# A two-layer trunk of sparse attention, retention and gated ConvFFN on one core: retention's loads a head ahead, the last FFN by the first one's code, and signs on ScalarE in the top-k

## The chip, the cores and the metric

One Trainium2 chip, one of its cores. TensorE (PE) multiplies, VectorE (DVE), ScalarE (ACT) and GpSimd (POOL) work on tiles of 128 partitions, SyncE (SP) issues the DMAs in order. The metric is device time in microseconds (us) from the first to the last instruction of one execution, as the median of several runs. Every product is made of float32 operands split into a high and a low fp32r part (three matmuls: high by high, high by low, low by high).

## The reference

```
for i in range(2):                                    # x: (1, 1024 tokens, 1024)
    h = rms_norm(x, norm_mix_g[i])
    x = x + (dsa_mixer(h) if i == 0 else retention_mixer(h))
    x = x + conv_ffn(rms_norm(x, norm_ffn_g[i]))

dsa_mixer:  proj = h @ w_in -> q (8 heads of 128), c (latent), qi, ki (8 index heads of 64), wi
    score = sum_h wi_h * relu(qi_h . ki), keys of later 64-chunks masked
    idx = top_k(score, 256);  k_sel, v_sel = gathered rms_norm(c), c
    o = softmax(q . k_sel) @ v_sel;   return o @ w_out
retention_mixer:  q, k = rotary(...) (4 heads of 256), v (4 of 512), g
    s = (q . k) * decay within chunks of 64; the state carries k^T v from chunk to chunk
    y = rms_norm(intra + cross) * silu(g);   return y @ w_out
conv_ffn:  u = causal 3-tap conv(h @ w_up) + bias -> a, b (2816 each);  return (silu(a) * b) @ w_down
```

## The kernel before, in words

Tokens are worked in two halves of 512, and activations lie with features on partitions. The large products over all tokens (FFN up, retention's q, k, g and values) are done by a Strassen-like scheme of seven products with operands B (first half) and T1 to T4, B22 (made of both halves by `second_inputs`). The first two products per chunk (`first_products`) need only the first half and can be made early; their results go out to DRAM (`pd`, `rp`) and come back in `second_products`.

Order of the stages: in_proj of half 0 and half 1, attention of query blocks 0 to 3, out_proj, part of the first FFN's first products, attention of blocks 4 to 7, out_proj, the first FFN, retention's inputs (`ret_inputs`: q, k, g by first and second products, then the values), retention half 0 and half 1, the second FFN (`ffn_whole`).

The top-k (L392) finds for each query the 256th largest score. It settles the 31 bits of a threshold from the top: one round counts per block, on DVE, the scores at or above the threshold (L407), then two small instructions set the bit (L417, L418). Top-k "a" is for blocks 2 and 3 (rows of 384 and 512 scores) and runs beside in_proj of half 1; top-k "b" is for blocks 4 to 7 (640, 768, 896, 1024) and runs beside the attention of blocks 0 to 3. Both are generators: other code draws a count or two at each of its own steps (`steps`, L1342, L1352), which sets where the counts stand in DVE's order.

The values (L605 and after, `run`): for each of two pairs of heads five products, each by two halves; a half's weight is summed on DVE, split on ACT and DVE, and multiplied. The loop asks for a weight where it is used.

Retention (L671) is called per half and loops over four heads: q·k (L730), the split of its masked result to sTh and sTl, in half 1 the state's load and split (L745), the output before the norm (rt), in half 0 the new state (L780 to L794), the next head's q and k (`qk`, L796: load through the raw buffers, rotary on DVE, split), transposes (L804) and the swish gate to y (L806), the next head's v (L809), then the head's part of the output product (L817) with weights by `weight()` (L97), which loads two ahead. There are two raw buffers (L84, L680), and q, k, v and weights all take them in turn.

`ffn_whole` makes the first products of four chunks in advance, the rest chunk by chunk. `down` takes its groups and tile places per layer from DOWN; in the first FFN the second half's convolution is done late, by `gate` (L1140).

Of the kernel before, what the change touches and what calls it, by code (L numbers as in the profile page):

```python
# [8 lines left out]
I32 = mybir.dt.int32  # L9
AF = mybir.ActivationFunctionType  # L10
# [5 lines left out]
T = 1024  # L16
# [3 lines left out]
DOWN = (([(0, 4), (4, 6), (10, 6), (16, 6)], (14,)), ([(0, 6), (6, 6), (12, 6), (18, 4)], (0, 12)))  # L20

PRE = (5, 4)
# [3 lines left out]
MASKED = -1.0e30  # L26

# [24 lines left out]
class Prog:  # L52
# [4 lines left out]
    def plan_weights(self, phases):  # L57
        i = self.ins
        seq = []
        for ph, a in phases:  # L60
# [5 lines left out]
            elif ph == "up":  # L66
                seq += [(i["wf_up"][0, c], 1024, True) for c in range(*a)]
            elif ph == "ret":
# [301 lines left out]
    def indexer(self, b, qs, t0, masks):  # L370
# [4 lines left out]
        for h in range(8):  # L375
            for (o, n) in self.segs(L):
# [6 lines left out]
                if h == 0:  # L383
                    nc.vector.tensor_scalar(sc[:, o:o + n], rl[:, :n], w, None, op0=ALU.mult)
# [7 lines left out]
    def topk(self, tag, scs, junk, eqs):  # L392

        nc = self.nc
# [6 lines left out]
        t = thr.bitcast(F32)  # L403

        def count(of, op):
            for b in range(B):
                V.tensor_scalar(junk[:, :Ls[b]], scs[b], of(b), None, op0=op, op1=ALU.add, accum_out=cnt[:, b:b + 1])  # L407
                yield
# [151 lines left out]
    def ret_inputs(self, x, tt, s3, B):  # L560
# [5 lines left out]
        def steps():  # L566
            yield
            yield
            self.mean_square(1)
            yield  # L570
            yield
            chunk = self.normaliser(x[1], C_GMIX + 8, 1)
            yield from self.second_inputs(x[0], x[1], tt, chunk, hold)

        rest = steps()
# [24 lines left out]

        nxt = self.prep_b(self.ret_src(0)[1], self.raw_of(self.ret_src(0)[0]), s3)
        self.second_products(16, self.ret_src, ops, nxt, s3, self.rp, done)

        for vp in range(2):
            vs = [self.hp.tile([128, 2, 2048], F32, tag="h", name="va") for _ in range(2)]  # L605
            (a21, a22), (a11, a12) = [(v[:, 0], v[:, 1]) for v in vs]
            for q in range(2):
                for t, hd, kh in ((a21, 1, 0), (a22, 1, 1), (a11, 0, 0), (a12, 0, 1)):
# [7 lines left out]
            def run(ps, of, tok, first, last, out):  # L616
# [3 lines left out]
                for j in range(4):  # L620
                    out(j, ps[j])
# [847 lines left out]
```

## Time and profile before

| | |
|---|---|
| median of 3 runs | 2869.95 us (2869.47 to 2870.96) |
| the profiled execution | 2871.95 us, span 2870.2 us |
| mean granted TensorE clock | 0.952 of full speed |
| PE busy | 2631.9 us (92%) |
| DVE busy | 2011.2 us (70%) |
| ACT busy | 1134.0 us (40%) |

Windows give the busy time of each engine in a stretch of the span, then PEclk, the granted clock as a share of full speed, and the share of DMA. Waits say which operation an engine stood before, and which engine's result it waited for last. Groups by shape read: line, engine, operation, out<-in, shapes, count | busy us, mean ns of one | idle before, by releaser. Stages by time: in_proj of half 1 from about 97, attention of blocks 0 to 3 from about 242, the first FFN's second part from 680, values 1600 to 1737, retention 1737 to 2194.3, the inputs of the second FFN 2194 to 2260.

### The profile page before, as it was taken

To read this page: it belongs to the slowest core of one execution; us is meant where nothing else is said; L and a number is where in the kernel's file an instruction comes from. 1 tells how busy PE (TensorE), PEld (TensorE's weight loads), DVE (VectorE), ACT (ScalarE), POOL (GpSimd) and SP (SyncE) were. 2 spreads that over 40 slices of the span, in tenths; PEclk is the share of its full clock that TensorE was granted. 3 is DMA by queue.
4 is the path that set the end of the run, shared out by engine and by line. 5 is a ranking of instruction groups with operands and counts; after the bars stand their busy time and mean duration, and the time that the engine had idled before them with its cause. 6 is when DMAs were issued, how large, how long until landed. Compare 5 with 4: busy or idle time off the path is not lost.

```text
span 2870.2 us, 31665 instructions
## 1 busy us (share of the span) xinstructions
PE 2631.9 (92%) x11616; PEld 2144.4 (75%) x11616; DVE 2011.2 (70%) x3036; ACT 1134.0 (40%) x1606; POOL 265.0 (9%) x193
## 2 busy tenths in 40 slices
PE   8977789998999999999999795896888999999999
PEld 6755567876888778888888674775676788888887
DVE  6889998766988778673566455657665977777633
ACT  6545434744433333354322113344333654444210
POOL 2543333311000000000000000000000000000000
PEclk9987889999999999999999897998899999999999
DMA  5211035123565665456555435333332333337722
GB/s 190 84 60 52 4 128 183 53 66 123 201 197 187 223 218 172 143 168 208 190 191 187 158 122 172 117 103 130 105 118 81 110 118 110 105 115 262 251 63 85
DMA packets 147212, 398.63 MB, mean 139 GB/s; under 512 B 16496, under 2 KB 17904, under 8 KB 147056
## 3 DMA queue, kind: packets, MB, share of 16 engines
q1 hardware_dynamic: 147056, 396.61, 41.5%
q8 instruction: 91, 1.49, 0.2%
q14 instruction: 65, 0.53, 0.1%
HBM read 280.68 MB, written 112.20 MB: 137 GB/s over the span
## 4 chain that ended last, share of the span: by engine, by line
PE 74%; DVE 17%; DMA 4%; issue 2%; ACT 2%; SPq 0%; POOL 0%; DVEq 0%; ACTq 0%; POOLq 0%
PE bank L849 35%; PE bank L125 11%; PE bank L126 10%; PE bank L124 10%; DVE junk L407 5%; PE bank L668 5%; DMA gin<-ud 1%; DVE tkb L417 1%; DVE t L860 1%; PE bank L535 1%; DVE tkt L418 1%; DMA wraw<-vd 1%; DVE x L835 1%; DVE sc L386 1%; DMA wraw<-in_wf_up 1%
## 5 line engine op out<-in xcount | busy, mean ns | idle before, releaser
L849 PE MATMUL bank<-B,whi 128*128 128x512 f32 x1440 | 445.4, 392 | 11.1 <-ACT B L826 4.1
L849 PE MATMUL bank<-T,whi 128*128 128x512 f32 x1344 | 419.5, 394 | 23.9 <-ACT T L826 16.0
L849 PEld LDWEIGHTS bank<-B,whi 128*128 128x128 f32 x1440 | 271.5, 189 | 69.8 <-ACT B L826 4.4
L849 PEld LDWEIGHTS bank<-T,whi 128*128 128x128 f32 x1344 | 254.5, 190 | 83.1 <-ACT T L826 18.1
L826 ACT ACTIVATE whi<-wraw 128x1024 fp32r<-128x1024 f32 (+2 forms) x178 | 169.5, 953 | 346.0 <-PE bank L125 159.1
L849 PE MATMUL bank<-B,wlo 128*128 128x512 f32 x720 | 278.4, 391 | 0.0
L125 PE MATMUL bank<-g,whi 128*128 128x512 f32 x704 | 273.6, 389 | 0.0
L126 PE MATMUL bank<-g,wlo 128*128 128x512 f32 x704 | 271.9, 389 | 0.5 <-DVE wlo L827 0.5
L124 PE MATMUL bank<-g,whi 128*128 128x512 f32 x704 | 266.1, 391 | 6.9 <-ACT g L826 5.2
L849 PE MATMUL bank<-T,wlo 128*128 128x512 f32 x672 | 262.7, 392 | 0.0
L827 DVE TENSOR_TENSOR wlo<-wraw,whi 128x1024 fp32r<-128x1024 f32 (+2 forms) x178 | 193.8, 1089 | 89.2 <-ACT whi L826 89.0
L88 ACT ACTIVATE whi<-wraw 128x1024 fp32r<-128x1024 f32 (+1 forms) x122 | 128.5, 1053 | 260.0 <-PE bank L125 90.4
L849 PE MATMUL bank<-T,wb 128*128 128x512 f32 x864 | 213.9, 391 | 0.8 <-DVE cu L860 0.8
L860 DVE TENSOR_TENSOR cu<-bank,t 128x512 f32<-128x512 f32 x198 | 133.9, 686 | 112.4 <-PE bank L849 107.3
L849 PEld LDWEIGHTS bank<-T,wb 128*128 128x128 f32 x864 | 163.1, 189 | 35.3 <-DVE cu L860 1.2
L407 DVE TENSOR_SCALAR_CACHE_REDUCE junk<-sc,tkt 128x640 f16<-128x640 f32 (+1 forms) x192 | 181.1, 943 | 4.4
L90 DVE TENSOR_TENSOR wlo<-wraw,whi 128x1024 fp32r<-128x1024 f32 (+1 forms) x79 | 97.6, 1238 | 115.6 <-ACT whi L88 112.0
L860 DVE TENSOR_TENSOR xo<-xo,bank 128x512 f32<-128x512 f32 x128 | 86.6, 683 | 123.4 <-PE bank L126 123.4
L124 PEld LDWEIGHTS bank<-g,whi 128*128 128x128 f32 x704 | 132.1, 188 | 35.6 <-ACT g L826 6.5
L849 PEld LDWEIGHTS bank<-B,wlo 128*128 128x128 f32 x720 | 135.9, 189 | 28.3
L126 PEld LDWEIGHTS bank<-g,wlo 128*128 128x128 f32 x704 | 132.1, 188 | 28.6 <-DVE wlo L827 1.0
L125 PEld LDWEIGHTS bank<-g,whi 128*128 128x128 f32 x704 | 132.1, 188 | 27.5
(257 smaller groups left out, 5167.4 us busy)
## 6 DMA issues: line engine op xcount, KB each, us to landing
wraw<-in_wf_up SPq DMA_DIRECT2D x113, 512.0 KB, 3.7
ud<-cu SPq DMA_DIRECT2D x88, 512.0 KB, 2.7
gin<-ud SPq DMA_DIRECT2D x88, 512.0 KB, 4.3
wraw<-in_wf_dn SPq DMA_DIRECT2D x56, 384.0 KB, 3.3
gd<-cu SPq DMA_DIRECT2D x32, 512.0 KB, 4.7
wraw<-in_wb_out SPq DMA_DIRECT2D x32, 512.0 KB, 3.7
wraw<-in_wa_in SPq DMA_DIRECT2D x26, 512.0 KB, 4.0
wraw<-in_wb_qk SPq DMA_DIRECT2D x24, 512.0 KB, 4.1
```

The costliest lines, as they stand in the source:

```text
L88: nc.scalar.activation(hi[:, :n], raw[:, :n], AF.Copy)
L90: eng.tensor_tensor(lo[:, :n], raw[:, :n], hi[:, :n].bitcast(F32), ALU.subtract)
L124: mm(ps, ah, bh, start=first, stop=False)
L125: mm(ps, ah, bl, start=False, stop=False)
L126: mm(ps, al, bh, start=False, stop=last)
L386: nc.vector.scalar_tensor_tensor(sc[:, o:o + n], rl[:, :n], w, sc[:, o:o + n], op0=ALU.mult, op1=ALU.add)
L407: V.tensor_scalar(junk[:, :Ls[b]], scs[b], of(b), None, op0=op, op1=ALU.add, accum_out=cnt[:, b:b + 1])
L668: self.nc.tensor.matmul(ps[j], u, v, start=first and k + i == 0, stop=k == 3 and i == 2, skip_group_check=True)
L826: return (self.nc.scalar.activation(hi, raw, AF.Copy), self.nc.vector.tensor_tensor(lo, raw, hi.bitcast(F32), ALU.subtract))
L827: self.nc.vector.tensor_tensor(lo, raw, hi.bitcast(F32), ALU.subtract))
L849: self.nc.tensor.matmul(ps, u, v, start=first and k + i == 0, stop=k == 3 and i == 2, skip_group_check=not (first and last))
L860: self.nc.vector.tensor_tensor(o, a, b, op)
```

## The change

- Top-k: the largest block of each top-k (512 and 1024 scores) is counted on ScalarE in 30 of 31 rounds, as the sum of the signs of score minus threshold (L438), turned into a count by a Copy (L439). For that the scores' bits are turned once before and back after. The small blocks are counted on DVE as before.
- The values: 20 half-steps in a list, weights made two half-steps ahead; the first two stand before the last chunk of g is finished.
- Retention: both halves in one loop of 8 heads. A head's q, k and v come to a tile of their own (`head`, 2 MB), asked for a head ahead. Rotary runs in that tile, in pieces between the rows of rt; its splits and the next state's stand between the output products. One of the two state products, or a group of output products held over from the head before, stands on each side of the transposes.
- The last FFN runs by the code of the first: all 22 chunks' first products in advance (weights by `weight()`), second inputs made beside them, late convolution in `down`. Both layers take T4 last of the T tiles and share one DOWN.

```diff
-DOWN = (([(0, 4), (4, 6), (10, 6), (16, 6)], (14,)), ([(0, 6), (6, 6), (12, 6), (18, 4)], (0, 12)))
...
+DOWN = ((0, 4), (4, 6), (10, 6), (16, 6))
+DOWN_H = (14,)
...
+        z, L = B - 1, Ls[B - 1]
+        half = self.stat.tile([128, 1], F32, tag=f"kh{tag}", name="tkh")
+        xi = scs[z].bitcast(I32)
+        x0 = scs[z].bitcast(U8)[:, 0::4]
+        low, signs = eqs.bitcast(U8)[:, :L], eqs.bitcast(I8)[:, 1024:1024 + L]
...
+        def count(of, op, to=B):
+            for b in range(to):
...
+        V.tensor_scalar(thr[:, z:], thr[:, z:], -(1 << 31), None, op0=ALU.bitwise_xor)
+        V.tensor_scalar(low, x0, 1, None, op0=ALU.bitwise_and)
+        yield
+        V.tensor_scalar(xi, xi, 1, None, op0=ALU.bitwise_or)
+        V.scalar_tensor_tensor(xi, xi, 31, xi, op0=ALU.logical_shift_right, op1=ALU.bitwise_xor)
+        yield
         for k in range(30, -1, -1):
-            yield from count(lambda b: t[:, b:b + 1], ALU.is_ge)
+            if k:
+                nc.scalar.activation(signs, scs[z], AF.Sign, bias=t[:, z:], accum_out=half)
+                nc.scalar.activation(cnt[:, z:], half, AF.Copy, bias=L / 2, scale=0.5)
+            yield from count(lambda b: t[:, b:b + 1], ALU.is_ge, B - 1 if k else B)
             V.tensor_scalar(bit, cnt, TOPK - 0.5, float(1 << k), op0=ALU.is_lt, op1=ALU.mult)
             V.scalar_tensor_tensor(thr, bit, (1 << k) >> 1, thr, op0=ALU.bitwise_xor, op1=ALU.bitwise_xor)
+            if k == 1:
+                V.tensor_scalar(thr[:, z:], thr[:, z:], -(1 << 31), None, op0=ALU.bitwise_xor)
+                V.scalar_tensor_tensor(x0, x0, 254, low, op0=ALU.bitwise_and, op1=ALU.bitwise_or)
+                yield
...
+        steps, half_steps = self.value_steps(ops)
+
+        def before_last():
+            half_steps[0]()
...
+        self.second_products(16, self.ret_src, ops, nxt, s3, self.rp, done, before_last)
+        for i, (prod, out) in enumerate(steps):
+            if i + 2 < len(steps):
+                half_steps[i + 2]()
+            else:
+
+                if i + 2 == len(steps):
+                    hd = self.head(0, 0)
+                    for _ in self.rotary(hd, self.uq[:, 4], self.uq[:, 5]):
+                        pass
+            prod()
+            if i + 1 < len(steps):
+                out()
+        return hd, out
...
+                    def make(p=p, q=q, of=of, w=w, vp=vp, load1=load1, load2=load2, load3=load3):
+                        if (vp, p, q) == (0, 0, 0):
+                            load1()
+                        if p == 0 and q == 1:
+                            load3()
+                        if (vp, p, q) == (0, 1, 0):
+                            load2()
+                        w["w"] = self.val_weight(of(q))
+                        if vp == 0 and q == 1 and p == 3:
+                            self.next_loads[0]()
+                        if vp == 0 and q == 1 and p == 4:
+                            self.next_loads[1]()
+
...
+    def head(self, half, n):
+
+        hd = self.hp.tile([128, 8, 512], F32, tag="h", name="hd")
+        sl = slice(half * H, half * H + H)
+        for d in (2, 3, 0, 1):
+            self.nc.sync.dma_start(hd[:, d], self.gd[0][n * 4 + d][:, sl])
+        for j in range(4):
+            self.nc.sync.dma_start(hd[:, 4 + j], self.vd[n][half][j])
+        return hd
+
+    def rotary(self, hd, cos, sin):
+
+        add = self.add
+        for o in (2, 0):
+            a, b = hd[:, o], hd[:, o + 1]
+            u, v = self.tmp(), self.tmp()
+            add(u, b, sin, ALU.mult)
+            yield
+            add(v, a, sin, ALU.mult)
+            yield
+            add(hd[:, o:o + 2], hd[:, o:o + 2], cos.unsqueeze(1).to_broadcast([128, 2, 512]), ALU.mult)
+            yield
+            add(a, a, u, ALU.subtract)
+            yield
+            add(b, b, v)
+            yield
...
+        split_two(2, "k")
+        split_two(0, "q")
+        split_v()
+        tail()
...
+        self.prefetch(1)
+        x = load_x()
+        items = [(half, n) for half in range(2) for n in range(4)]
+        held = None
+        for it, (half, n) in enumerate(items):
+            nxt = items[it + 1] if it + 1 < len(items) else None
...
+            sg = self.l1.tile([128, 4, 512], F32, tag="sg", name="sg")
+            for c in range(4):
+                nc.sync.dma_start(sg[:, c], self.gd[1][n * 4 + c][:, half * H:half * H + H])
+            if nxt:
+                hd = self.head(*nxt)
...
-            if n < 3:
-                nxt = qk(n + 1)
-            elif then:
-                next(then)
+                    yield
...
+            other = state() if half == 0 else held
+            next(other)
             y = self.ogp.tile([128, 2, 4, 512], F32R, tag="og", name="y")
...
-            for mm in range(4):
+                self.split(y[:, 0, c], y[:, 1, c], t)
+            next(other)
+
+            def out(mm, half=half, n=n, y=y):
...
+            for mm in range(4):
+                if mm == 3 and (half, n) in ((0, 3), (1, 0), (1, 1), (1, 2)):
+                    held = out(3)
+                else:
+                    for _ in out(mm):
+                        pass
...
+                if nxt:
+                    if mm == 0:
+                        for _ in turn:
+                            pass
+                        split_two(2, "k")
+                    elif mm == 1:
+                        split_two(0, "q")
+                    elif mm == 2:
+                        split_v()
+                        load_state(*nxt)
...
-        T1, T2, T4, B22, T3 = [tt.tile([128, 2, 4, 512], F32R, tag="T", name=n) for n in ("T1", "T2", "T4", "B22", "T3")]
+        T1, T2, B22, T3, T4 = [tt.tile([128, 2, 4, 512], F32R, tag="T", name=n) for n in ("T1", "T2", "B22", "T3", "T4")]
...
+    def later_inputs(self, x, gc, tt, hold):
+
+        yield
+        yield
+        self.mean_square(1)
+        yield
+        yield
+        chunk = self.normaliser(x[1], gc, 1)
+        yield from self.second_inputs(*x, tt, chunk, hold)
+
+    def ffn_second(self, x, tt, s3):
+        hold = []
+        rest = self.later_inputs(x, C_GFFN + 8, tt, hold)
+        src = self.up_src(1)
+        for i, _ in enumerate(self.first_products(range(NFF), self.B, self.pd)):
+            next(rest, None)
+            if i == 2 * NFF - 2:
+                nxt = self.prep_b(src(0)[1], self.raw_of(src(0)[0]), s3)
+        self.ffn(1, tt, s3, hold[0], nxt)
+
+    def ffn(self, l, tt, s3, ops, nxt):
+        nc = self.nc
+        late = lambda c: c >= DOWN[0][1]
...
```

The order shows three places. First top-k a, beside in_proj of half 1. Before, on DVE (junk is the count's unused output, tkc the counts, tkb and tkt the bit and the threshold):

```order
L407 TENSOR_SCALAR junk,tkc<-sc,tkt 128x384
L407 TENSOR_SCALAR junk,tkc<-sc,tkt 128x512
L417 TENSOR_SCALAR tkb<-tkc 128x2
L418 SCALAR_TENSOR_TENSOR tkt<-tkb,tkt 128x2
L407 TENSOR_SCALAR junk,tkc<-sc,tkt 128x384
L407 TENSOR_SCALAR junk,tkc<-sc,tkt 128x512
L354 SCALAR_TENSOR_TENSOR s_1434<-msq,bank 128x32
L417 TENSOR_SCALAR tkb<-tkc 128x2
L418 SCALAR_TENSOR_TENSOR tkt<-tkb,tkt 128x2
```

After, on DVE:

```order
L422 TENSOR_SCALAR junk,tkc<-sc,tkt 128x384
L441 TENSOR_SCALAR tkb<-tkc 128x2
L442 SCALAR_TENSOR_TENSOR tkt<-tkb,tkt 128x2
L422 TENSOR_SCALAR junk,tkc<-sc,tkt 128x384
L144 SCALAR_TENSOR_TENSOR t_1495<-bank,cols,t_1494 128x512
L441 TENSOR_SCALAR tkb<-tkc 128x2
L442 SCALAR_TENSOR_TENSOR tkt<-tkb,tkt 128x2
L422 TENSOR_SCALAR junk,tkc<-sc,tkt 128x384
```

And after, on ACT for the same rounds (eqs is the signs' unused output, tkh their sum; L96 splits a weight, L240 and L241 belong to in_proj):

```order
L438 ACTIVATE eqs,tkh<-sc,tkt 128x512
L439 ACTIVATE tkc<-tkh 128x1
L438 ACTIVATE eqs,tkh<-sc,tkt 128x512
L96 ACTIVATE whi<-wraw 128x1024
L439 ACTIVATE tkc<-tkh 128x1
L240 ACTIVATE t_1488<-bank 128x512
L438 ACTIVATE eqs,tkh<-sc,tkt 128x512
L241 ACTIVATE t_1489<-t_1488 128x512
L439 ACTIVATE tkc<-tkh 128x1
```

The 128x512 count left DVE. On ACT a Sign and a Copy came, with other work of ACT between them in about half of the rounds.

Second SP's queue in retention's half 0. Before, around the second head (sg the gate's rows, vd the values, wraw the two raw buffers, gd q and k):

```order
L754 DMA sg<-gd_6_244 128x512
L754 DMA sg<-gd_7_245 128x512
L682 DMA wraw<-vd_0_0_270 128x512
L682 DMA wraw<-vd_0_1_271 128x512
L682 DMA wraw<-vd_0_2_272 128x512
L682 DMA wraw<-vd_0_3_273 128x512
L87 DMA wraw<-in_wb_out 128x1024 x6
L682 DMA wraw<-gd_10_232 128x512
```

After, at the first head's end of loading (x_6 and x_7 the last rows of the second half's residual, hd the tile of a coming head):

```order
L1462 DMA x<-xr_6_188 128x512
L1462 DMA x<-xr_7_189 128x512
L839 DMA sg<-gd_1_239 128x512
L839 DMA sg<-gd_2_240 128x512
L839 DMA sg<-gd_3_241 128x512
L95 DMA wraw<-in_wb_out 128x1024 x2
L770 DMA hd<-gd_10_232 128x512
L770 DMA hd<-gd_11_233 128x512
```

Values and q, k no longer pass through wraw; the weights stand there alone, and the first head's last three sg pieces stand behind x. Third, DVE around a head's transposes in half 0. Before (L806 makes y before its split, `y<-t,y` is the low part, kf and the raw buffers hold k and q under rotary):

```order
L860 TENSOR_TENSOR t_13834<-wraw,cs 128x512
L860 TENSOR_TENSOR t_13835<-wraw,cs 128x512
L806 SCALAR_TENSOR_TENSOR t_13852<-bank,cols,sg 128x512
L806 SCALAR_TENSOR_TENSOR t_13861<-bank,cols,sg 128x512
L860 TENSOR_TENSOR kf<-kf,t_13818 128x512
L860 TENSOR_TENSOR wraw<-wraw,cs 128x512 x2
L860 TENSOR_TENSOR t_13834<-t_13834,t_13835 128x512
L860 TENSOR_TENSOR wraw<-wraw,cs 128x512
L806 SCALAR_TENSOR_TENSOR t_13870<-bank,cols,sg 128x512
L806 SCALAR_TENSOR_TENSOR t_13879<-bank,cols,sg 128x512
L827 TENSOR_TENSOR y<-t_13852,y 128x512
L827 TENSOR_TENSOR y<-t_13861,y 128x512
```

After (hd is the next head's tile, L897 the norm's small step, kl and ql the low parts of k and q, L921 the gate):

```order
L995 TENSOR_TENSOR hd<-hd,t_13836 128x512
L995 TENSOR_TENSOR hd<-hd,t_13837 128x512
L962 TENSOR_TENSOR kl_13972<-hd,kh_13971 128x1024
L897 SCALAR_TENSOR_TENSOR s_13839<-s_13833,kon 128x1
L962 TENSOR_TENSOR ql_14010<-hd,qh_14009 128x1024
L897 SCALAR_TENSOR_TENSOR s_13860<-s_13857,kon 128x1
L921 SCALAR_TENSOR_TENSOR t_13887<-bank,cols,sg 128x512
L921 SCALAR_TENSOR_TENSOR t_13896<-bank,cols,sg 128x512
L921 SCALAR_TENSOR_TENSOR t_13905<-bank,cols,sg 128x512
L921 SCALAR_TENSOR_TENSOR t_13914<-bank,cols,sg 128x512
L962 TENSOR_TENSOR y<-t_13887,y 128x512
L962 TENSOR_TENSOR v<-hd,v 128x1024 x2
```

The rotary and the splits of k and q moved ahead of the four gate products; before, they stood among them.

## Rows read from the trace of the kernel before

**Rows 1.** Page, part 1: each engine's busy us, share of the span, instructions.

```profile
PE 2631.9 (92%) x11616; PEld 2144.4 (75%) x11616; DVE 2011.2 (70%) x3036; ACT 1134.0 (40%) x1606; POOL 265.0 (9%) x193
```

**Rows 2.** Windows: stretch, length, busy us (instructions) per engine, PEclk, DMA share, GB/s.

```profile
97.00:188.00 91.00, 71.27 (x305) 52.91 (x304) 86.97 (x218) 32.93 (x53) 52.71 (x25) 0.90 0.32 90
...
242.00:340.00 98.00, 64.48 (x216) 44.62 (x217) 95.96 (x279) 44.38 (x99) 30.79 (x38) 0.65 0.06 22
...
720.00:980.00 260.00, 260.00 (x1148) 215.29 (x1148) 221.21 (x278) 98.22 (x100) 0.00 (x0) 1.00 0.59 195
980.00:1080.00 100.00, 92.60 (x396) 74.79 (x395) 74.14 (x82) 34.21 (x36) 0.00 (x0) 0.98 0.66 226
```

**Rows 3.** Windows of the retention, the values before it, the inputs behind it.

```profile
1737.00:2194.30 457.30, 363.48 (x1594) 295.77 (x1594) 280.97 (x476) 177.91 (x318) 19.83 (x33) 0.89 0.36 118
1600.00:1737.00 137.00, 115.52 (x484) 93.34 (x482) 68.49 (x76) 22.26 (x21) 0.00 (x0) 0.91 0.35 128
2194.00:2260.00 66.00, 53.56 (x224) 41.35 (x223) 55.99 (x71) 33.58 (x43) 1.01 (x1) 0.90 0.24 79
```

**Rows 4.** Timeline of PE, consecutive products of 512 columns behind a wait.

```profile
1893.11 0.63 PE L124 MATMUL bank<-y,whi 128*128 128x512 f32 x1
1893.54 0.63 PE L125 MATMUL bank<-y,whi 128*128 128x512 f32 x1
```

**Rows 5.** PE's waits, 1737 to 2213: us in total, times, longest.

```profile
PE bank L124 <- ACT whi L88: 36.9, 4, 19.8
PE bank L124 <- ACT qh L826: 18.8, 2, 11.3
PE bank L125 <- DVE stl L827: 11.1, 3, 7.5
PE bank L124 <- ACT sth L826: 8.3, 4, 4.0
PE bank L125 <- DVE y L827: 8.3, 6, 3.3
PE bank L124 <- ACT y L826: 6.4, 6, 1.4
```

**Rows 6.** Timeline of SP's queue in the first head: start, us, issue.

```profile
1778.83 4.96 SPq L682 DMA_DIRECT2D wraw<-vd  x4
1787.03 1.98 SPq L87 DMA_DIRECT2D wraw<-in_wb_out  x2
```

**Rows 7.** PE's waits, 1590 to 1737.

```profile
PE bank L668 <- ACT whi L826: 21.5, 4, 15.5
```

**Rows 8.** PE's waits, 2194 to 2262.

```profile
PE bank L849 <- ACT T L826: 9.8, 3, 7.8
PE bank L849 <- DVE T L827: 2.4, 2, 2.0
```

**Rows 9.** Timeline of DVE: the last instructions of two rounds of top-k a.

```profile
99.56 0.16 DVE L418 SCALAR_TENSOR_TENSOR tkt<-tkb,tkt 128x2 int32<-128x2 int32 x1
...
101.40 0.16 DVE L418 SCALAR_TENSOR_TENSOR tkt<-tkb,tkt 128x2 int32<-128x2 int32 x1
```

**Rows 10.** DVE's groups by shape, 60 to 500: busy us, mean ns of one.

```profile
L407 DVE TENSOR_SCALAR_CACHE_REDUCE junk<-sc,tkt 128x1024 f16<-128x1024 f32 x32 | 40.8, 1275 | 0.5
...
L407 DVE TENSOR_SCALAR_CACHE_REDUCE junk<-sc,tkt 128x384 f16<-128x384 f32 x32 | 19.6, 611 | 1.0
...
L417 DVE TENSOR_SCALAR tkb<-tkc 128x2 int32<-128x2 f32 x31 | 19.8, 638 | 1.0
```

**Rows 11.** ACT's groups by shape, whole span.

```profile
L502 ACT ACTIVATE lg<-lg,s,sq 128x1024 f32<-128x1024 f32 x8 | 9.9, 1236 | 5.9 <-DVE s L500 5.9
...
L502 ACT ACTIVATE lg<-lg,s,sq 128x512 f32<-128x512 f32 x8 | 6.5, 813 | 10.5 <-DVE s L500 10.5
...
L502 ACT ACTIVATION_READ_ACCUMULATOR lg<-lg,s,sq 128x1 f32 x64 | 12.0, 187 | 0.0
...
L88 ACT ACTIVATE whi<-wraw 128x1024 fp32r<-128x1024 f32 x120 | 127.1, 1059 | 256.4 <-PE bank L125 88.3 <-DMA wraw<-in_wb_out 54.0 <-PE bank L849 53.5
```

More of the change, by code (lines that the diff above doesn't have):

```diff
@@ L564, in ret_inputs @@
         hold = []
[L566 to L575, printed above, removed]
+        rest = self.later_inputs(x, C_GMIX + 8, tt, hold)
         for _ in self.first_products(range(16), B, self.rp):
@@ L651, in ret_inputs, with keep, f @@
[L651 to L652 removed]
+                    r, w = self.tmp(), t[which[0]][:, which[1] + j]
+                    add(r, ps, w)
+                    nc.sync.dma_start(self.vd[n][half][j], r)
+                return f
+            def keep(dst, o, t=t):
+                def f(j, ps):
+                    add(t[dst][:, o + j], ps, t["pq"][:, j])
+                return f
@@ new lines, in value_steps, with prod, after @@
+            banks = {}
+            seq = (("d", s1, T1, True, False, keep("pq", 4)), ("a", s2, T2, True, False, keep("uq", 0)),
+                   ("d", s4, B22, False, True, give(2 * vp, 1, ("uq", 0))),
+                   ("a", s3, T3, False, False, give(2 * vp + 1, 1, ("pq", 4))),
+                   ("a", a22, T4, False, True, give(2 * vp + 1, 0, ("pq", 0))))
+            for p, (to, of, tok, first, last, out) in enumerate(seq):
+                for q in range(2):
+                    w = {}
+                    def make(p=p, q=q, of=of, w=w, vp=vp, load1=load1, load2=load2, load3=load3):
[10 more added lines that the diff above has]
+                            self.next_loads[1]()
+                    def prod(q=q, to=to, tok=tok, first=first, last=last, w=w, banks=banks):
+                        if first and q == 0:
+                            banks[to] = [self.bank() for _ in range(4)]
+                        self.val_product(banks[to], *w.pop("w"), tok, q, first, last)
+                    def after(q=q, to=to, out=out, banks=banks):
+                        if q == 1:
+                            for j in range(4):
+                                out(j, banks[to][j])
+                    prep.append(make)
+                    steps.append((prod, after))
@@ L711, in values @@
             v = self.ogp.tile([128, 2, 4, 512], F32R, tag="og", name="v")
             for j in (0, 2):
-                raw = raw_pair([self.vd[n][half][j + i] for i in range(2)])
-                self.split(self.two(v, 0, j), self.two(v, 1, j), raw)
-            return v[:, 0], v[:, 1]
-        nxt = qk(0)
-        nxtv = values(0)
-        for n in range(4):
-            qh, ql, kh, kl, kf = nxt
-            vh, vl = nxtv
+                self.split(self.two(v, 0, j), self.two(v, 1, j), flat(hd[:, 4 + j:6 + j]))
@@ new lines, in split_v, with load_state @@
+            cur["v"] = v[:, 0], v[:, 1]
+        def load_state(half, n):
+            if half == 1:
+                sth = self.l1.tile([128, 2, 512], F32R, tag="sh", name="sth")
+                stl = self.l1.tile([128, 2, 512], F32R, tag="sl", name="stl")
+                for d in range(2):
+                    st = self.tmp()
+                    nc.sync.dma_start(st, self.state[n * 2 + d])
+                    self.split(sth[:, d], stl[:, d], st)
+                cur["st"] = sth, stl
+        split_two(2, "k")
@@ L772, in retention @@
                 nc.scalar.activation(rt[:, j], ps, AF.Square, accum_out=ss)
+                for _ in range((2, 2, 2, 1)[j]):
+                    next(turn, None)
                 ms = self.small(1)
```

335 lines of the change are left out of this document (127 added, 208 removed).

## The prediction

> **What bounds the kernel now.** I read the page's busy shares first, then windows by stage, then what PE waits for in the weak stages, then the timelines at the longest waits. PE is busy for 2631.9 of 2870.2 us [rows 1]. From 720 to 980 it never stops: 1148 matmuls in 260.00 us, .2265 us each, at a granted clock of 1.00 [rows 2]. The change leaves PE's work as it is (11,544 matmuls and 5.59 million columns in both programs), so what can be won is time in which PE idles or runs at its lower clock.
>
> Windows show where that is. In the retention PE is busy 363.48 of 457.30 us at a clock of 0.89; in the values before it 115.52 of 137.00; in the second layer's FFN inputs behind it 53.56 of 66.00 [rows 3]. During top-k b PE is busy 64.48 of 98.00 at 0.65 while DVE is busy for 95.96; in top-k a 71.27 of 91.00, DVE 86.97 [rows 2]. Those two are DVE's stages, the three others are stages of waits.
>
> The clock costs beside the waits. [...] The retention's 1594 products, by width, take about 328 us at the full rate (an estimate: 1274 of 512 columns at .2265 are 289, the narrower 320 the rest), so of the 129 us lost there 94 are idle and 35 are clock.
>
> **The retention.** PE's waits there are 36.9 us for a split output weight, 18.8 for the first q·k operands, 11.1 and 8.3 for the state's split, 8.3 and 6.4 for y [rows 5]; some 4 more are small. The weights come late since SP gives its two raw buffers to q, k, v and weights in turn: the two output weights of the first head are issued at 1787.03, behind four pieces of v [rows 6]. After the change heads come into tiles of their own, a head ahead, and raw buffers hold weights alone; q, k and v of head 0 are split ahead of the values' end, and the next head's state is split before its turn. So the first four waits go: 36.9 + 18.8 + 11.1 + 8.3 = 75.1. If the low clock goes with its idle time, 35 × 75/94 = 28 goes too.
>
> What is late next: y. All rotary pieces and both splits now stand on DVE ahead of y's four products, and their two splits between small steps of the norm. Against that, a held product group and the state's product stand on PE around the transposes. I take 1.5 us more for each of 8 heads, 12. Three pieces of sg of head 0 stand behind 4 MB of x on SP, where x takes two buffers that the values still use: 3 us; and 3 for the start itself. Net −75 −28 +18 = −85. Bounds: if y is covered wholly, half of its 14.7 us goes as well and nothing new comes, −111; if half of what goes turns up at another place, 52, and head 0 waits 7 more, −45.
>
> **The values.** PE's waits for split weights are 21.5 us in 4 pieces, the longest 15.5 [rows 7]: each sum on DVE and its split on ACT starts when the last product is under way. After the change 20 half-steps have their weights made two ahead, the first two beside the last g product. I take 21.5 and 2.5 of the clock: −24. Bounds: −27 (all of the loss) and −15 (the first, where loads queue behind g's stores).
>
> **The last FFN's inputs.** T's splits make PE wait 9.8 and 2.4 us [rows 8], on top of a clock of 0.90 [rows 3]. After it, 44 first products, two for each chunk, run while the second inputs are made, as in the first FFN. Their results make a trip through DRAM; DMA is busy a fifth to a third there [rows 3], so I cost that at nothing; if it shows, it is in the bounds. −14 (of 17 lost), bounds −8 and −17.
>
> **Its down products** start as the first FFN's do, with the second convolution late, and that stretch is 92.60 busy of 100.00 for 396 matmuls [rows 2], which at .2265 are 89.7: 10 us that the last FFN did not pay. The T tiles, now taken in another order in both layers, give some of it back (an estimate): +6, bounds −6 and +10.
>
> **Top-k a.** An undisturbed round is 1.84 us (99.56 to 101.40, [rows 9]), and 31 rounds fill most of 91 us [rows 2], 2.7 to 2.9 each: DVE's small steps stall (.638 us where .17 is usual, [rows 10]) and other work of DVE stands between. One count, .75 by the slope between the 384 and the 1024 row [rows 10], goes from each round; a Sign with a sum comes to ACT. No row shows Sign; the nearest is Exp with a sum: .813 + .187 at 512 columns, 1.236 + .187 at 1024 [rows 11]. Then a one-column Copy, for which I take .19 as for the read, and the two small steps: 1.0 + .2 + .33 and hops of .3 in all make 1.85, while DVE's own part is 1.1. So the chain over ACT is as long as the round was, and it now also carries what ACT holds in between. In the order after, 14 of 30 rounds have another ACT instruction between Sign and Copy (17.4 us at their means), and 15.5 us stand between Copy and the next Sign. I take a third of these 33 us, less the little that a round gains elsewhere, and the passes over the largest block that turn its bits and back (five, about .75 each by the count's price) are in it: +10; bounds −22 (.75 × 30, nothing lost) and +33.
>
> **Top-k b.** DVE is rid of 30 × 1.275 us [rows 10]. The other three counts are about 3.0 us by the slope between the 384 and the 1024 row, so ACT's 1.24 + .19 + .2 and hops fit beside them. But rounds are drawn per step of the attention: by the order, 26 rounds in place of 21 now stand ahead of the next block's input splits, and DVE's work up to there sums to 174.9 us at the means, against 176.1. The time freed comes where PE is full already. −4; bounds −26 (30 × 1.275 × 21/31) and 0. Together top-k is +6, bounds −48 and +33.
>
> [...]
>
> **The sum.** −85 −24 −14 +6 +6 = −111 on a span of 2870.2. The profiled execution took 2871.95 (1.75 outside its span), the median of the three runs 2869.95, 2.0 less. 2871.95 − 111 − 2.0 = 2759 us. All ends together reach from −209 (2661) to −25 (2845).
>
> **Rivals.**
> 1. More is won: ACT's counts cost top-k nothing (−22 in place of +6) and y is covered (−111 in place of −85): 2759 − 28 − 26 = 2705. For it: DVE at 95.96 of 98.00 with PE's clock at 0.65 in top-k b [rows 2]. Against it: the rounds refill DVE. 0.14.
> 2. The retention keeps half of its waits, since y waits behind DVE's larger block of rotary work and hd lands late behind x: −45 in place of −85, 2799. For it: DVE is busy 280.97 us there and loses little, about 11 by the order at the means; y already waits in 12 places [rows 5]. Against it: the weights' 36.9 have a cause that is gone. 0.15.
> 3. Slower: ScalarE and VectorE hand each of 60 rounds to and fro, in order on both, and each round waits for whatever ACT holds (a bank PE has not filled, a weight buffer PE has not freed). The place is L439's Copy, and the next block's inputs hang on the last round. The other terms give −117, so it decides from 117/60 = 1.95 us a round; at 2.5 us the time is 2869.95 − 117 + 150 = 2903. For it: 88.3 us of splits waiting for PE [rows 11]. Against it: top-k b has DVE work of 3 us beside each Sign, so mostly the 30 rounds of a are exposed. 0.04.
> 4. It does not do what it says: the retention's loads only change which one is late (0 in place of −85) and top-k pays 33 as at its bound in place of 6; the rest gives −24 −14 +6 = −32: about 2871. 0.03.
>
> **How the numbers follow.** The forecast has 0.64, with 2715 to 2805 for itself. Adding the upper half of the first rival's spread and most of the second's: 2705 to 2812 for 8 in 10. Faster by over 0.2% (about what this kernel's runs tell from no change): 0.64 + 0.14 + 0.15 = 0.93. Within: 0.02 of the last case; slower: 0.05, the third and the rest of the fourth.
>
> **What would show it.** Waits of PE for a split output weight under 5 us and for first q·k operands under 4; PE idle in the retention 20 to 40 us, clock 0.95 or more; waits for value weights under 3; waits for T in the last FFN near none, and a start of its down products that idles like the first's; top-k a's rounds at about 3.1 us, with DVE idle for ACT's Copy; top-k b's stretch about as long as before. Wrong it is if y's waits come to over 30 us, if ACT's Copy leaves DVE idle in top-k b too, or if the values wait on loads.

## The result: 94 us faster, and the profile after

The changed kernel takes 2776.45 us (median of 4 runs, 2775.69 to 2779.98) against 2870.45 for the kernel before beside it: a ratio of 0.9672, 95% interval 0.9655 to 0.9689. The forecast was 2759, the range 2705 to 2812. The profiled execution has a span of 2774.8 us, 95.4 less than before. The page's first part, to be held against [rows 1]: PE is less busy in sum for the same 11616 products (its mean granted clock is 0.969 in place of 0.952), and ACT has the signs.

```profile
PE 2612.7 (94%) x11616; PEld 2130.3 (77%) x11616; DVE 1959.9 (71%) x2918; ACT 1162.4 (42%) x1722; POOL 278.1 (10%) x193
```

Where the time went: stages cut where PE starts the first product of each, in the traces of four kernels (two are experiments below). The lost time is the length less the stage's columns at .2265 us per 512. Two things about the retention's row: in before and signs_only, 24 first products of the last FFN (5.4 us) stand inside it, which in the other two stand behind it; and its 176 products of 128 columns start .109 us apart in the traces (as the eleven from 1770.58 on in that of before), where this rate gives .057, so about 9 us of its loss, in every column, is no loss (an estimate from these starts).

| stage, us (lost) | before | signs_only | after | no_signs |
|---|---|---|---|---|
| to the attention | 239.2 (53) | 240.9 (55) | 242.0 (56) | 238.0 (52) |
| attention 0 to 3 | 99.7 (69) | 93.1 (62) | 93.5 (62) | 99.5 (69) |
| output projection, B | 61.3 (14) | 70.4 (24) | 70.5 (24) | 62.8 (16) |
| first FFN's first products | 94.8 (10) | 102.1 (17) | 102.1 (17) | 95.5 (11) |
| attention 4 to 7, to the T products | 188.6 (27) | 188.7 (27) | 188.7 (27) | 188.4 (27) |
| first FFN's second products | 313.9 (18) | 324.4 (28) | 324.6 (28) | 314.0 (18) |
| first down | 251.8 (9) | 255.8 (13) | 256.3 (14) | 252.8 (10) |
| retention's inputs | 367.0 (18) | 367.5 (19) | 348.4 (2) | 348.7 (3) |
| values | 132.0 (23) | 131.5 (23) | 115.0 (4) | 114.8 (3) |
| retention | 445.5 (129) | 445.5 (129) | 361.7 (50) | 359.1 (48) |
| last FFN up to down | 433.1 (19) | 433.1 (19) | 421.4 (4) | 421.8 (5) |
| last down | 243.2 (4) | 243.2 (4) | 250.8 (9) | 254.4 (13) |

Windows of the changed kernel for the retention, the values and the stretch behind the retention answer to [rows 3] (same columns): PE's clock is 0.97 in place of 0.89, and in the other two it is 1.00.

```profile
1741.00:2102.70 361.70, 337.01 (x1568) 277.37 (x1569) 262.76 (x431) 163.81 (x298) 33.19 (x33) 0.97 0.42 141
1626.00:1741.00 115.00, 112.13 (x493) 92.22 (x493) 76.27 (x89) 26.23 (x26) 0.00 (x0) 1.00 0.61 212
...
2102.70:2222.00 119.30, 119.30 (x535) 98.88 (x534) 56.84 (x63) 56.55 (x80) 1.01 (x1) 1.00 0.58 193
```

PE's waits from 1737 to 2110, against [rows 5]. The split output weight's 36.9 us are 0.2 and not among these rows; y keeps 7.6, and one wait for the state is left, at the first head of half 1:

```profile
PE bank L132 <- ACT y L961: 7.6, 6, 1.7
PE bank L132 <- ACT sth L961: 6.1, 1, 6.1
PE bank L919 <- ACT rt L900: 3.3, 4, 1.4
PE bank L189 <- DVE acc L183: 2.3, 1, 2.3
PE bank L132 <- ACT sTh L861: 2.1, 1, 2.1
PE bank L132 <- ACT qh L961: 2.1, 1, 2.1
```

Top-k's two stretches, against [rows 2]: in a, DVE's 87 busy us are 58 and PE is no faster; in b, DVE is as full as before.

```profile
97.00:188.00 91.00, 72.08 (x296) 53.81 (x295) 57.68 (x154) 58.61 (x140) 51.25 (x25) 0.88 0.31 90
...
242.00:340.00 98.00, 65.48 (x239) 45.93 (x238) 97.16 (x290) 65.03 (x148) 30.80 (x38) 0.74 0.08 27
```

What DVE does in a instead is wait for ScalarE's Copy. First its waits from 97 to 188, then one round on ACT (start, us): between the Sign and its Copy stand two copies of banks, 1.0 us, and VectorE's next step follows at 113.68 after 2.15 us of idling.

```profile
DVE tkb L441 <- ACT tkc L439: 25.8, 24, 3.2
```

```profile
111.81 0.71 ACT L438 ACTIVATE eqs<-sc,tkt 128x512 int8<-128x512 f32 x1
112.42 0.19 ACT L438 ACTIVATION_READ_ACCUMULATOR eqs<-sc,tkt 128x1 f32 x1
112.51 0.57 ACT L354 ACTIVATE t<-bank 8x512 f32<-8x512 f32 x1
112.99 0.57 ACT L240 ACTIVATE t<-bank 128x512 f32<-128x512 f32 x1
113.47 0.18 ACT L439 ACTIVATE tkc<-tkh 128x1 f32<-128x1 f32 x1
```

```profile
113.68 0.24 DVE L441 TENSOR_SCALAR tkb<-tkc 128x2 int32<-128x2 f32 x1 [2.15 <-ACT tkc L439]
```

The next Signs, at 114.22 and 115.97, have no such work between them and stand 1.75 us apart, with .37 for VectorE's L441; from the one at 129.47, where L441 takes .16, to the next it is 1.59. An undisturbed round on VectorE alone took 1.84 [rows 9].

By the starts of L441, a's 31 rounds take 2.81 us each (2.69 before), b's 5.83 (6.83 before). B's last round starts at 434.3 in place of 460.0, and yet the second attention starts at 508.0 in place of 495.0. Between the two PE waits for the sum of squares behind the output projection. Before (338 to 495) and after (335 to 508):

```profile
PE bank L181 <- DVE acc L175: 4.0, 1, 4.0
```

```profile
PE bank L189 <- DVE acc L183: 12.3, 1, 12.3
```

PE is done with that projection 2 us earlier than before (384.3 against 386.6), but the last of VectorE's sums ends 6 us later (396.6 against 390.5), and the first split of B starts at 409.8 in place of 403.0: 26 rounds stand ahead of it in place of 21, and their small step L441 is slower. The groups of that step from the attention's start to the first split of B, before (239.2 to 403.03) and after (242 to 409.76):

```profile
L417 DVE TENSOR_SCALAR tkb<-tkc 128x4 int32<-128x4 f32 x21 | 4.3, 206 | 0.1
```

```profile
L441 DVE TENSOR_SCALAR tkb<-tkc 128x4 int32<-128x4 f32 x26 | 13.5, 521 | 0.7
```

Ten of the 26 take over .3 us, three of the 21 before. Each of these thirteen runs beside an instruction of GpSimd and ends within .05 us of the end of one. This one ends at 375.73, GpSimd's split of an output weight at 375.70:

```profile
374.59 1.14 DVE L441 TENSOR_SCALAR tkb<-tkc 128x4 int32<-128x4 f32 x1
```

```profile
373.30 2.40 POOL L98 TENSOR_TENSOR wlo<-wraw,whi 128x1024 fp32r<-128x1024 f32 x1 [3.10 <-PE bank L133]
```

That the step is held by GpSimd fits all of them; no run takes GpSimd's work away to show it. Part of this only changed place: the seven sums themselves (acc) took 8.2 us before and take 4.8 now.

### The profile page after: what moved, and what is told of

Same layout as the page of the kernel before. It is cut to its first block, busy times and chain, and to the rows that moved or that the text cites. A ratio compares the mean times of both kernels' runs of the same rounds, so it can differ in the third digit from the quotient of the medians.

```text
span 2774.8 us, 32038 instructions
## 1 busy us (share of the span) xinstructions
PE 2612.7 (94%) x11616; PEld 2130.3 (77%) x11616; DVE 1959.9 (71%) x2918; ACT 1162.4 (42%) x1722; POOL 278.1 (10%) x193
## 4 chain that ended last, share of the span: by engine, by line
PE 70%; DVE 16%; DMA 6%; issue 3%; ACT 3%; POOL 1%; SPq 1%; DVEq 0%; ACTq 0%; POOLq 0%
PE bank L984 35%; PE bank L132 10%; PE bank L133 9%; PE bank L134 9%; PE bank L762 5%; DVE junk L422 3%; DMA gin<-ud 2%; DMA wraw<-in_wf_up 1%; DVE tkb L441 1%; DVE wlo L962 1%; PE bank L563 1%; DVE t L995 1%; DVE sc L394 1%; DVE tkt L442 1%; ACT eqs L438 1%
## 5 line engine op out<-in xcount | busy, mean ns | idle before, releaser
L984 PE MATMUL bank<-T,wb 128*128 128x512 f32 x1368 | 338.9, 391 | 6.0 <-DVE wb L962 2.4
L984 PE MATMUL bank<-T,whi 128*128 128x512 f32 x1008 | 314.8, 394 | 11.1 <-ACT T L961 5.8
L984 PEld LDWEIGHTS bank<-T,wb 128*128 128x128 f32 x1368 | 258.1, 189 | 62.6 <-DVE wb L962 3.7
L132 PE MATMUL bank<-g,whi 128*128 128x512 f32 x704 | 265.1, 395 | 14.3 <-ACT g L961 13.2
L96 ACT ACTIVATE whi<-wraw 128x1024 fp32r<-128x1024 f32 (+1 forms) x144 | 151.6, 1053 | 250.9 <-PE bank L133 103.1
L98 DVE TENSOR_TENSOR wlo<-wraw,whi 128x1024 fp32r<-128x1024 f32 (+1 forms) x101 | 123.8, 1226 | 185.2 <-ACT whi L96 133.4
L961 ACT ACTIVATE whi<-wraw 128x1024 fp32r<-128x1024 f32 (+2 forms) x143 | 132.2, 925 | 286.7 <-DVE wraw L995 140.9
L984 PEld LDWEIGHTS bank<-T,whi 128*128 128x128 f32 x1008 | 191.0, 190 | 55.2 <-ACT T L961 6.8
L984 PE MATMUL bank<-T,wlo 128*128 128x512 f32 x504 | 198.0, 393 | 0.2 <-DVE wlo L962 0.2
L962 DVE TENSOR_TENSOR wlo<-wraw,whi 128x1024 fp32r<-128x1024 f32 (+2 forms) x143 | 150.9, 1055 | 17.9 <-ACT whi L961 17.7
L995 DVE TENSOR_TENSOR wraw<-wraw 128x512 f32<-128x512 f32 x180 | 123.7, 687 | 3.0
```

Of the source, the lines that this page charges most:

```text
L96: nc.scalar.activation(hi[:, :n], raw[:, :n], AF.Copy)
L98: eng.tensor_tensor(lo[:, :n], raw[:, :n], hi[:, :n].bitcast(F32), ALU.subtract)
L132: mm(ps, ah, bh, start=first, stop=False)
L961: return (self.nc.scalar.activation(hi, raw, AF.Copy), self.nc.vector.tensor_tensor(lo, raw, hi.bitcast(F32), ALU.subtract))
L962: self.nc.vector.tensor_tensor(lo, raw, hi.bitcast(F32), ALU.subtract))
L984: self.nc.tensor.matmul(ps, u, v, start=first and k + i == 0, stop=k == 3 and i == 2, skip_group_check=not (first and last))
```

## Experiments

Medians are of 4 or 5 runs; each ratio is to the kernel before, run beside it.

**The signs, taken out and put in alone.** no_signs is the changed kernel with this undone, and the turning of the bits with it (of the change's edits to the top-k only a constant of -2^-100 added to the scores stays):

```diff
...
-                nc.scalar.activation(signs, scs[z], AF.Sign, bias=t[:, z:], accum_out=half)
-                nc.scalar.activation(cnt[:, z:], half, AF.Copy, bias=L / 2, scale=0.5)
-            yield from count(lambda b: t[:, b:b + 1], ALU.is_ge, B - 1 if k else B)
+            yield from count(lambda b: t[:, b:b + 1], ALU.is_ge)
```

> The changed kernel with all counts of the top-k on VectorE, as before the change. Theory: the signs cost 13 us in the stretch from the attention to the second attention (its start moved from 495.0 to 508.0) and, since VectorE's order in the first FFN's second products differs only where the signs are in (by the order, this kernel has the old one again), 11 us there as well: 2776 - 24 = 2752, within 5. Rival one, the new order of the T tiles causes the 11 us in the first FFN: 2763. Rival two, the signs pay, since top-k b's last round came 26 us earlier with them: 2785 or more.

2751.97 us, 0.9582 (0.9568 to 0.9597): 24 faster than the changed kernel, as the theory had it. signs_only is the kernel before with the same lines, their preparation and the constant put in.

> The kernel before with the signs on ScalarE alone added, nothing else of the change. Theory: 2870 + 13 + 11 = 2894, within 6, with VectorE's new order in the first FFN's second products and waits of PE there. Rival one (T order causes the FFN's part): 2883. Rival two (the signs pay): under 2870.

2897.74 us, 1.0093 (1.0078 to 1.0108). Both table columns give the same picture from two sides: 2 to 4 us lost up to the attention, 6 won in it, 8 or 9 + 7 lost behind it, 10.5 in the first FFN's second products, 4 in its down products. The signs are a loss of 24 to 27 us inside a change that gains 119 elsewhere.

**Which top-k.** signs_a and signs_b keep the signs in one of the two; this is signs_a's edit, and signs_b's is the same for top-k a.

```diff
-                gens.append(self.topk("b", [masks[b] for b in (4, 5, 6, 7)], *junk))
+                gens.append(self.topk_dve("b", [masks[b] for b in (4, 5, 6, 7)], *junk))
```

> The changed kernel with the signs in top-k a alone; top-k b counts on VectorE as before. By the order, VectorE's instructions of the first FFN's second products are then the old ones. Theory: a's rounds are handed to and fro between ScalarE and VectorE for 3 us more and nothing else moves: 2752 (no signs) + 3 = 2755. Rival (the signs of a also bring the later losses): 2765 or more.

> The changed kernel with the signs in top-k b alone. By the order, VectorE's instructions of the first FFN's second products are then the new ones, and 27 rounds stand ahead of the first B split, as in the changed kernel. Theory: all but a's 3 us of the signs' cost is here: 2776 - 3 = 2773, with the wait of 12 us for the sum of squares behind the output projection and 28 us lost in the first FFN's second products. Rival (a's signs bring it): 2756 or less.

2759.98 us (0.9614, 0.9601 to 0.9627) and 2771.80 (0.9654, 0.9641 to 0.9668). Signs in a cost 8, more than the 3 expected: 5 up to the attention, and 5 in the last down products, far from it, that I can't explain (that stage took 250.8 to 259.3 us in the traces of six kernels with the same code there). Up to the attention the traces without signs in a take 237.8 to 240.0 us, those with them 240.7 to 245.1, so a loss there is clear and its size is not. The first FFN's second products take 313.9 us with signs in a and 323.7 with signs in b; so that loss comes with b's.

**Rounds kept from going ahead.** signs_held7, where `held` is the last split of B on VectorE, behind which what the block draws is issued:

```diff
-                x[0] = self.out_proj(0, *ot, lambda m: steps(5))
+                x[0] = self.out_proj(0, *ot, lambda m: steps(7))
...
-                    steps(3)
-                steps(200)
+                    with tc.issue_after(held):
+                        steps(3)
+                with tc.issue_after(held):
+                    steps(200)
```

> The changed kernel with one edit in what the rounds of top-k b stand ahead of: the rounds that are not drawn by the output projection (7 steps each) are issued on VectorE behind the last split of B. By the order, 17 rounds stand ahead of the first B split in place of 27; the first FFN's second products have the new order still. Theory: the 12.3 us wait for the sum of squares falls to 3 or less and the attention's 6 us stay won, the first FFN's 11 us stay lost: 2776 - 9 - 3 = 2764. Rival (what is put off comes back, the masks of blocks 4 to 7 come late): 2776 or more.

2767.80 us (0.9641, 0.9628 to 0.9654), 9 less than the changed kernel. PE's wait for the sum of squares, in its trace from 330 to 500:

```profile
PE bank L189 <- DVE acc L183: 3.9, 1, 3.9
```

The trace has 17 rounds ahead of the first split of B, the sign's round counted in (27 in the changed kernel), and VectorE's last sum ends at 386.7. The rounds that VectorE's free time had drawn in front of the output projection's sums made that wait. The second attention starts at 494.8, but takes 112.9 us up to its output projection in place of 108.5: part of what was put off came back.

**The order in the first FFN.** conv_after moves the convolution passes behind the sums on the next raw weights:

```diff
-            done(c, cc)
...
+                    with tc.issue_after(self.last_sum.ins):
+                        done(held[0], held[4])
```

> The changed kernel, signs and all; in both FFNs' second products the convolution passes of a chunk are issued on VectorE behind the last sum on the raw weights of the next, so that by the order these sums mostly stand together again, as before the change. Theory: VectorE's order there is what costs 10.7 us in the first FFN (a raw buffer comes free later, the next weights are asked for later): its second products take 314 us in place of 324.6, 2776 - 11 = 2765. Rival (the loss there has another cause, such as what the signs leave behind in buffers): 2774 or more.

2811.69 us (0.9794, 0.9778 to 0.9811): the theory fell. The stage took 336.7 us, not 314, and the last FFN up to its down products 444.5 in place of 421.4. VectorE's wait for raw weights in these stages (the kernel before 707 to 987, the changed one and conv_after 720 to 1000):

```profile
DVE t L860 <- DMA wraw<-in_wf_up: 0.5, 1, 0.5
```

```profile
DVE t L995 <- DMA wraw<-in_wf_up: 12.6, 7, 4.2
```

```profile
DVE t L995 <- DMA wraw<-in_wf_up: 41.8, 12, 5.1
```

PE loses 17.6, 28.3 and 37.7 us there in the same order. What matters seems to be what stands behind a sum whose weights have not landed: VectorE waits at it, and passes that were ready wait with it. In the changed kernel one such sum waits 2.09 us, to 745.73, and a pass whose input ScalarE had finished at 745.32 runs behind it, at 747.54. The stage's time goes with its order: VectorE has the old one, row for row, in before, no_signs, signs_a and held_off, with 314 us each, and the other in after, signs_only, signs_b and signs_held7, with 324. But in these runs the order of ScalarE's instructions and of SyncE's loads there moves with VectorE's, and the new order never comes without signs in b, so which of them costs the 10.5 us stays open. That such an edit of order costs time by itself is shown in conv_after's last FFN, 23 us, a layer whose code the signs do not touch; that it acts by this wait is what fits the three rows, not more.

> The best that the signs can be given by these findings: signs in top-k b alone, its later rounds issued behind the last B split (20 rounds ahead of the first, 8 steps drawn by the output projection), and the convolution passes behind the sums as in conv_after. Theory: 2772 (signs_b) - 9 - 10 = 2752, the same as without signs (2752), since what the attention gains, 6 us, goes in the stretch behind it. Rival (the attention's 6 us stay): 2746 or less.

2804.75 us (0.9769, 0.9752 to 0.9785), by the same fault of conv_after (338.5 and 325.1 us in the two layers' second products). Its earlier stages do bear on the question: the attention takes 93.5 us, 6 less than without signs, and the second one starts at 496.3, where it is 495.8 without signs. What top-k b gains does not reach it.

**The raw buffers.** raw_own, on the kernel before (`own` is one tile of 128 x 4 x 1024):

```diff
-            raw = self.wp.tile([128, 1024], F32, tag="raw", bufs=2, name="wraw")
+            if half == 0:
+                raw = own[:, len(used) % 4]
+                used.append(1)
+            else:
+                raw = self.wp.tile([128, 1024], F32, tag="raw", bufs=2, name="wraw")
```

> The kernel before with one edit: in retention's half 0, q, k and v are loaded into a tile of four pairs of their own, and the two raw buffers hold weights alone; when they are asked for is as before. Theory: PE's waits for a split output weight in half 0, 25.7 us in 3 pieces, go, and the low clock behind them in proportion (35 of 94): 2870 - 35 = 2835, within 8; the wait of 11.3 us for the first q operands stays. Rival, the weights are late because the transfers are slow or SP issues them late anyway: 2862 or more.

2845.57 us (0.9913, 0.9897 to 0.9930), 26 less, between the theory and its rival. PE's waits in half 0, before (1740 to 1963) and in raw_own (1740 to 1935):

```profile
PE bank L124 <- ACT whi L88: 25.7, 3, 19.8
PE bank L124 <- ACT qh L826: 11.3, 1, 11.3
PE bank L125 <- DVE y L827: 6.9, 3, 3.3
PE bank L124 <- ACT y L826: 2.7, 3, 0.9
```

```profile
PE bank L124 <- ACT qh L833: 12.7, 1, 12.7
PE bank L125 <- DVE y L834: 10.0, 4, 3.3
PE bank L124 <- ACT y L833: 3.4, 4, 1.0
```

The 25.7 us for weights are gone, so sharing the raw buffers was their cause. The windows from the first product of q and k to the end of half 0, before and in raw_own:

```profile
1748.30:1963.50 215.20, 179.11 (x792) 146.04 (x792) 128.76 (x223) 87.89 (x161) 9.44 (x16) 0.89 0.37 121
```

```profile
1748.10:1935.20 187.10, 172.80 (x792) 141.79 (x792) 120.32 (x218) 80.49 (x156) 9.40 (x16) 0.95 0.36 121
```

The stretch is 28 us shorter: 25.7 of waits for weights, and 6 of clock where 9.6 were expected (PE is busy 6.3 us less for the same products, the clock 0.95 in place of 0.89), less 4 that the waits for y grew. The first q operands are still waited for, 12.7 us here and 7.5 at the start of half 1, as before (11.3 and 7.5). In the changed kernel, with loads a head ahead, 2.1 of them are left.

**What covers y.** held_off is no_signs with nothing held for the transposes:

```diff
-            other = state() if half == 0 else held
-            next(other)
+            for _ in (state() if half == 0 else ()):
+                pass
...
-                if mm == 3 and (half, n) in ((0, 3), (1, 0), (1, 1), (1, 2)):
-                    held = out(3)
-                else:
-                    for _ in out(mm):
-                        pass
+                for _ in out(mm):
+                    pass
```

> The kernel without signs, and in the retention no product is held for the transposes: both state products stand ahead of them, and the last output group of a head stands in its own head. Theory: y is what is late next; its wait of about 1.4 us a head grows by most of the 2.7 us of the group that stood behind the transposes, 8 times, with some low clock behind it: 2752 + 20 = 2772. Rival (y was never late by much, 14.7 us in all before the change): 2752 + 7 or less.

2762.11 us (0.9620, 0.9607 to 0.9633), 10 more. y's wait grew little (7.6 to 8.8), the norm's from 3.2 to 14.3. The retention of no_signs (1714 to 2075), then of held_off (1714 to 2085):

```profile
PE bank L900 <- ACT rt L881: 3.2, 4, 1.4
```

```profile
PE bank L900 <- ACT rt L881: 14.3, 17, 2.8
PE bank L132 <- ACT y L937: 8.8, 8, 1.2
```

The held products cover the rows of rt ahead of the transposes; the size is half of what I gave them, and the place another.

**The late convolution.** late_first is no_signs with it in the first FFN alone:

```diff
-        late = lambda c: c >= DOWN[0][1]
+        late = lambda c: l == 0 and c >= DOWN[0][1]
```

> The kernel without signs, and the second convolution of the last FFN is done beside its second products, as that layer had it before; only the first FFN does it late. Theory: the last down stretch lost 12.5 us in that kernel and 4.0 before the change, so 8 us come back there, but 36 passes of 1.28 us come to VectorE beside the second products, where it is busy 248 of 303 us: 294 of 303, and at least as much is lost there: 2752 to 2764. Rival (VectorE has room): 2744.

2757.94 us (0.9598, 0.9582 to 0.9615), 6 more, though the intervals overlap. The last FFN's second products and down products, in no_signs and then in its trace:

```profile
2192.60:2495.30 302.70, 299.73 (x1322) 247.58 (x1321) 247.59 (x312) 114.68 (x117) 0.00 (x0) 1.00 0.59 194
2495.30:2749.70 254.40, 246.53 (x1068) 202.27 (x1068) 161.49 (x176) 67.37 (x69) 0.00 (x0) 0.99 0.49 162
```

```profile
2196.20:2509.10 312.90, 304.41 (x1321) 246.08 (x1319) 281.29 (x341) 131.70 (x132) 0.00 (x0) 1.00 0.55 183
2509.10:2757.20 248.10, 242.87 (x1068) 200.37 (x1068) 126.23 (x146) 49.20 (x54) 0.00 (x0) 1.00 0.51 172
```

6.3 us come back in the down products, 10 go in the stage ahead of them.

**The T order.** no_signs_t_old puts T4 third again.

> As no_signs, and the T tiles in the order of before (T4 third). Theory: the tile order touches only the first groups of the down products, where the first FFN lost 13.5 us with the new order and 9.0 with the old: 4 to 9 us less than no_signs for both layers, 2745. Rival one: the tile order is what moved VectorE's order in the first FFN, then 11 us less than no_signs. Rival two: T4 last is worth its place, since T4 is used last: no_signs or some us more.

2751.50 us (0.9585, 0.9570 to 0.9599): no difference to no_signs, so it neither gives nor costs, and the first down's loss in the changed kernel comes with the signs.

Of all kernels run, no_signs and no_signs_t_old are the fastest, 24 us under the changed one and 119 under the one before.

## Why the prediction was right in the sum, and where a term failed

The retention and the values, −85 and −24: by the lost times of the table, retention's inputs, values and retention together went from 170 us to 56, −114 where −109 was forecast (the lengths, 944.5 to 825.1, give −119, but 5.4 of that are the last FFN's products that no longer stand there). The mechanism held: the four waits of 75.1 us [rows 5] are down to about 8 (6.1 for the state, 2.1 for q), the clock rose from 0.89 to 0.97, and raw_own shows the shared buffers as the weights' cause. That the sum came so near was in part luck. PE's idle time in the retention fell by 69 us (93.8 to 24.7) where the prediction has 57, 75 less the 18 of "new waits": y did not grow (7.6 and 0.8 against 14.7), and sg of head 0 behind x cost nothing that shows. That the clock costs beside the waits shows at [rows 4]: from 1893.00 to 1894.50 the trace has a granted clock of 0.50, and products start .43 us apart; from 1896 to 1900 it has 0.99, and they start .23 apart. But the clock gave back less than the 28 forecast: by the prediction's own count, some 35 us became 15. Rival 2, half of the waits kept, is out.

The last FFN, −14 and +6: by lost time −14 (18.7 to 4.4 us) and +5 (4.0 to 8.9); its lengths, −11.7 and +7.6, count products that moved between the stages. late_first shows the +6 as the price of an edit that saves 10 at another place.

Top-k, +6: this is the term that failed, and it more than makes up the 17 us between the forecast and the result. It measured +13 up to the second attention, and +15 behind it, in the first FFN's second products and down products, where my sum had nothing at all; no_signs and signs_only put the whole at 24 and 27. Top-k a was right in kind and high in size (+10 expected, +3 by the table): VectorE waits 24 times for the Copy, 25.8 us in all, but had 25 us less to count (30 counts at .745 and .08 for each one's read). The forecast's undisturbed round over ScalarE, 1.85 us, was near (1.59 and 1.75); the .3 for hops in it came from no row, and in the round at 129.47 the four gaps between its instructions make .25 (.03, .09, .04, .09). Other work does stand between a Sign and its Copy, 1.0 us of it in the round at 111.81; the whole of the 33 us, the term's upper bound, did not come. Top-k b failed in sign. I had "the time freed comes where PE is full already" and cost the refilling at nothing (−4). But the rounds that refill VectorE's order stand ahead of the output projection's sums, and these were waited for: −6 in the attention, +9 and +7 behind it. signs_held7 took 9 of them back.

The step that was wrong, then: I summed VectorE's work ahead of the B splits (174.9 against 176.1) and took an equal sum for an equal end. That sum is "at the means", and the small step's mean over all rounds of b is .317 us before. Ahead of the first split of B it was .206 before and .521 after, 4.3 us and 13.5, and that split came 7 us later, 3 of them since the attention itself began later. And I looked at the order where the change was made, not at the stages behind it, where the order had moved as well; how that order costs its 10.5 us stays open.

Small slips in the working, none of which moves the forecast: the .17 of a small step that does not stall stands in no line of [rows 10], but 19 of the 31 L417 of top-k a take .16 or .17; the weight splits waited for PE not 88.3 us but 141.8, since [rows 11] has 53.5 more under L849; and the traces have 11616 products, not 11,544.

## What to carry to other kernels

- Moving work to a second engine inside a chain that both take part in need not shorten a round: read the length of the round, not the busy time that it frees. In a VectorE's 87 us became 58 and the rounds went from 2.69 to 2.81 us; in b, where VectorE has 3 us of its own counts beside each Sign, they fell from 6.83 to 5.83, and the kernel still lost.
- Where a scheduler sets the order, compare the order in every later stage too: with an edit some 200 us upstream, a stage whose code had not changed took 10.5 us more.
- Where two kinds of loads take one pair of buffers in turn, give each its own: that alone won 26 us here. The waits for the first operands stayed until they were also asked for a step earlier.

## What the runs showed of the hardware

A Sign with a sum takes less than the Exp that I priced it by [rows 11]: 1.144 us at 1024 columns and .720 at 512, each with .187 for the sum's read; the one-column Copy takes .196. The groups on ACT from 60 to 520:

```profile
L438 ACT ACTIVATE eqs<-sc,tkt 128x1024 int8<-128x1024 f32 x30 | 34.3, 1144 | 28.7 <-DVE tkt L442 27.5 <-DVE s L528 0.9 <-DVE s L532 0.4
...
L438 ACT ACTIVATE eqs<-sc,tkt 128x512 int8<-128x512 f32 x30 | 21.6, 720 | 23.9 <-DVE tkt L442 20.4 <-DVE tkt L430 3.4
...
L439 ACT ACTIVATE tkc<-tkh 128x1 f32<-128x1 f32 x60 | 11.7, 196 | 0.9
...
L438 ACT ACTIVATION_READ_ACCUMULATOR eqs<-sc,tkt 128x1 f32 x60 | 11.2, 187 | 0.0
```
